# A conditioned hybrid decoder layer: nine pairs of up-projection tiles by half-size products in place of seven

## The chip, the cores and the metric

The kernel runs on one core of one Trainium2 chip. The metric is the device time of one execution in microseconds, as the median of several runs. A core has five engines that work side by side, each through its own list of instructions in order: TensorE (PE in the profile; its weight loads, PEld, overlap its products), VectorE (DVE), ScalarE (ACT), GpSimd (POOL) and SyncE (SP). SP, ACT and POOL also issue DMA transfers. Where an instruction needs what another engine or a transfer makes, it waits for a semaphore, and all that stands behind it in the same list waits too.

## The reference

One decoder layer on 512 tokens of width 1024, in float32. The part in front (conditioning, the input projection, two kinds of attention heads) is left out here. What matters is the end:

```python
mix = jnp.concatenate([o_hg, o_nsa], axis=-1) @ w_out[l]
x = x + gt1 * mix
h2 = rmsnorm(x, norm2_g[l]) * (1.0 + sc2) + sh2
u = causal_dwconv(h2 @ w_up[l], conv_w[l], conv_b[l])   # 1024 -> 5632, width 3
a, v = jnp.split(u, 2, axis=-1)
x = x + gt2 * ((jax.nn.silu(a) * v) @ w_down[l])        # 2816 -> 1024
```

`gt2` is one of six parts of `silu(c) @ w_ada + b_ada`, a row of 1024 numbers that the kernel spreads over 128 partitions. It is called the gate below.

## The kernel before

**Exact products from three.** A float32 operand is split into a rounded part `hi` (ACT copies it to a 32-bit format with fewer digits, L152) and the rest `lo` (DVE subtracts, L153). Each product of two such operands is three TensorE instructions (`mm3`, L155 to L158). Making `hi` and `lo` is called making a form. Some forms are made the other way ("added", L259 to L261 and L1694 to L1696): ACT writes the negated source into `lo`, and a DMA issued on POOL adds the source to it.

**The up-projection.** The 5632 output columns are 44 tiles of 128 columns, numbered `st` = 0 to 43. Two neighbours (an even one for `a`, an odd one for `v`) make one part `f` of the 22 parts of the hidden layer. A plain tile takes 8 blocks of the width by 3 products of 512 tokens, 24 products. After a tile, `up_post` (L1626) runs the width-3 convolution on ACT and DVE, the silu, and the product of the two.

From tile 8 on the tiles come in units of four (`j` is the unit's number, its tiles are `4j` to `4j+3`). In a unit the first two tiles are computed together by seven products of half size (a Strassen-Winograd scheme over halves of the width, of the tokens and of the two tiles). Tokens P1 to P7 stand for them. Each is 4 blocks by 3 products of 256 tokens, 84 in all in place of 96 half-size ones. They need sums of the inputs (`hS`, made once) and sums of the weights (`wq`, `e`, made for each unit by DVE). The other two tiles are plain, cut in two pieces each (tokens B0, B1, C0, C1).

**The order is written out by hand.** `PRO` (L46) is the order of the prologue (tiles 0 to 7) and `UNIT` (L47) that of a unit. Each token is a call in `do_` (L1745): M3 is the products of tile 3, q1 the `up_post` of tile 1, F6 and A5 the form of tile 6 and the added form of tile 5, p2 the `up_post` of the unit's third tile, m0' and m1' the forms of the next unit's two plain tiles, n1' to f7' the sums and forms of the next unit's weights, t a sum of inputs, x one item of the list `work`, g a step of the gate. An engine's instructions stay in the order in which the tokens make them. Before, units 2 to 8 come (`NU = 8`), and then a loop of eight plain tiles, 36 to 43, in which the digits of `PLAIN` say how many steps of the gate follow each tile.

**Work after a tile.** For each pair of parts, `g_parts` (L1818) puts sums and forms for the down-projection on the list `work`. `step` takes from it. The last item, `park` (L1845), stores what there is no room for in HBM. `gran`, the pool that holds most of this, has 33 slots, called granules. For the pairs named in `AWAY`, one more granule, `gQ`, is parked.

**The gate.** `ada_last` (L1399) is a generator. Each half of the gate is 8 blocks of 128 rows of `w_ada`, loaded one at a time (256 KB) and added up by DVE (L1410, L1415, L1420). Then comes a split into `hi` and `lo`, two products that add over the partitions (L1426, L1427) and a copy by ACT. In the first half each load goes into one buffer and so follows the DVE instruction that read the block before.

**The down-projection** also has seven products of half size, in four phases. `forms` (L1875) makes the forms of its weights, and `look` (L1930) asks for the next one, three ahead of the products. `each_a` (L2032) is what is done beside the first phase, the return of the parked granules among it (`load_away`, L1896; the third phase's `load_s34`, L1891).

Of the kernel before, what the change touches and what calls it, by code (L numbers as in the profile page):

```python
# [20 lines left out]
P = 128  # L21
T = 512
NT = T // P
D = 1024
# [17 lines left out]
NU = 8  # L42
AWAY = (0, 1)
CUT = {"B": 6, "C": 7}
ADD = (1, 1)
PLAIN = "2 A1 1 1 A2 1 1 1"  # L46
PRO = ("t t g x M1 M2 t t t t F3 M3 F4 t A5 q0 M4 q1 q2 F6 q3 M5 M6 A7 x q4 g x q5 x t x n1' ns' f2' nc' n5' q6 na' g s4' m0' x x M7 m1' x f6' f7' x x x x f4'")  # L47
# [64 lines left out]
def hybrid_layer_kernel(ctx: ExitStack, tc: tile.TileContext, d: dict, out: bass.AP, dbg=None):  # L112
# [1165 lines left out]
    def hg_mix(i):  # L1278
# [13 lines left out]
        rstd(r[:, 0:4], s[:, 0:4], 1.0 / P, 4.0 * EPS)  # L1292
        on = TMP([P, 4, P], tag="on")
# [4 lines left out]
    def hg_flip(i):  # L1298
# [10 lines left out]
        split(m[:, 0], m[:, 1], t)  # L1309
# [89 lines left out]
    def ada_last(s, res):  # L1399
        for q in range(2):  # L1400
            acc = res[:, q * 512:(q + 1) * 512]
            c0 = s * D + q * 512
            gp.memset(acc, 0.0)
            sp.dma_start(acc[0:1], d["b_ada"][:, c0:c0 + 512])
            for k in range(KT if q else 0):
                raw = TMP([P, 512], tag="ada2r")
                sp.dma_start(raw, ada_view[:, k, c0:c0 + 512])
                if k:
                    yield
                    ve.scalar_tensor_tensor(acc, last, cs[:, k - 1:k], acc, ALU.mult, ALU.add)  # L1410
                last = raw
            for k in range(0 if q else KT):
                last = res[:, 512:]
                if k:
                    ve.scalar_tensor_tensor(acc, last, cs[:, k - 1:k], acc, ALU.mult, ALU.add)  # L1415
                sp.dma_start(last, ada_view[:, k, c0:c0 + 512])
                if k < KT - 1:
                    yield
            yield
# [3 lines left out]
            split(hi, lo, acc)  # L1423
            yield
# [4 lines left out]
            yield  # L1429

# [146 lines left out]
    for i in range(NT):  # L1577
        x1.append(G([D], s="x1"))
        sp.dma_start(x1[i], x_view[:, i])
    next(gate1)  # L1580
# [6 lines left out]
    hg_mix(2)  # L1587
# [7 lines left out]
    hg_flip(2)  # L1595
# [20 lines left out]
    def up_mm(st, sl, ks=range(KT)):  # L1616
        if st not in us:
            us[st] = PS("u")
            if st not in wts:
                wts[st] = next_parts(st < nst - 2, added=st >= 4 * NU + 4 and PLAIN.split()[st - 4 * NU - 4][0] == "A")  # L1620
# [114 lines left out]
    def do(j, tok):  # L1735
        last = j == NU
        if tok.endswith("'"):
            if last:
                if tok in ("n1'", "m0'"):
                    piece()  # L1740
# [4 lines left out]
    def do_(j, tok):  # L1745
        lo_, hi_ = lo_half, hi_half
        w = forms7.get(j)
        u = partial(u_of, j)
        if tok == "P1":
            banks(j)  # L1750
            sprod(u(1, lo_), w[1], h2_quarter(0, lo_), True)
        elif tok == "P5":
# [25 lines left out]
        elif tok == "g":  # L1778
            next(ada2, None)
# [164 lines left out]
    gt2 = wp.tile([P, D], F32, tag="xin", name="gt2", bufs=1)  # L1944
# [165 lines left out]
```

## Time and profile before

| what | value |
|---|---|
| median of 3 runs | 674.73 us (674.34 to 675.54) |
| the profiled execution's own time | 674.35 us |
| its span, first to last instruction | 672.6 us |
| TensorE busy | 664.9 us (99%), 3999 products |
| VectorE busy | 577.8 us (86%) |
| ScalarE busy | 392.6 us (58%) |
| GpSimd busy | 60.0 us (9%) |
| moved by DMA | 128.52 MB, mean 191 GB/s |
| granted TensorE clock | 1.000 |

The stages by time from the start of the span: the attention heads end near 271 us; the output projection and the second normalization run to about 327 us; the up-projection's prologue to 372 us; seven units to 520 us; eight plain tiles to 564 us; the down-projection to 669 us.

How to read a row of the timeline: start in us, length in us, engine, line of the kernel, operation, output and inputs by the program's names, shape, count, and in brackets how long the engine had been idle and what ended that. The starts of neighbouring TensorE rows say what a product costs, since products overlap: the length of a row is longer than its step to the next. In the view by windows each row is one stretch: its length, then the busy time and count of instructions of PE, PEld, DVE, ACT and POOL, the granted clock, the share of time that the 16 DMA engines were busy, and GB/s.

### The profile page before, as it was taken

What the parts mean: (1) busy time and instruction counts of PE and PEld (TensorE: products, weight loads), DVE (VectorE), ACT (ScalarE), POOL (GpSimd) and SP (SyncE); (2) the same over time, 40 slices, a digit from 0 to 9 for tenths busy, and PEclk for the clock granted to TensorE, in tenths of its full rate; (3) what the DMA queues carried; (4) which work ended last, traced back from release to release, by engine and by line L of the source; (5) the groups of instructions that cost most, each with busy time, mean ns of one, the idle gap of its engine ahead of it and who ended that gap; (6) DMA issues with size and microseconds to landing.
All of it is one profiled execution on the core that took longest, in us unless ns stands there. A gap on an engine that the chain in (4) does not pass through costs nothing.

```text
span 672.6 us, 10869 instructions
## 1 busy us (share of the span) xinstructions
PE 664.9 (99%) x3999; PEld 565.1 (84%) x3999; DVE 577.8 (86%) x1155; ACT 392.6 (58%) x757; POOL 60.0 (9%) x80
## 2 busy tenths in 40 slices
PE   8999999999999999999999999999999999999998
PEld 4678898788898889888998888989888888888886
DVE  5688988999998997687878988998898789988787
ACT  5564446666677688335665766667675455553431
POOL 1006144200000000200000011010110000000000
PEclk9999999999999999999999999999999999999999
DMA  9998444388042132435436677986779773979932
GB/s 279 287 322 269 145 157 138 106 288 254 11 147 95 33 107 99 172 96 161 140 95 172 179 196 198 242 218 175 187 181 277 217 234 124 393 259 398 388 112 94
DMA packets 110473, 128.52 MB, mean 191 GB/s; under 512 B 7067, under 2 KB 84691, under 8 KB 110421
## 3 DMA queue, kind: packets, MB, share of 16 engines
q1 hardware_dynamic: 103541, 106.89, 51.1%
q0 software_dynamic: 2448, 8.91, 6.9%
q10 hardware_dynamic: 4432, 12.04, 4.7%
q8 instruction: 31, 0.51, 0.3%
q14 instruction: 21, 0.17, 0.1%
HBM read 105.01 MB, written 13.90 MB: 177 GB/s over the span
## 4 chain that ended last, share of the span: by engine, by line
PE 92%; SPq 3%; DMA 2%; DVE 1%; issue 0%; ACTq 0%; ACT 0%
PE u L156 11%; PE u L158 11%; PE u L157 11%; PE dn L157 5%; PE dn L156 5%; PE dn L158 5%; PE pT L156 3%; PE pT L158 3%; PE pT L157 3%; PE F L1059 3%; PE oT L1087 3%; PE oh L158 2%; PE oh L156 2%; PE oh L157 2%; SPq L317 2%; PE lev L1188 2%
## 5 line engine op out<-in xcount | busy, mean ns | idle before, releaser
L156 PE MATMUL u<-h2h,whi 128*128 128x512 f32 (+1 forms) x208 | 78.0, 375 | 0.0
L157 PE MATMUL u<-h2l,whi 128*128 128x512 f32 (+1 forms) x208 | 77.8, 374 | 0.0
L158 PE MATMUL u<-h2h,wlo 128*128 128x512 f32 (+1 forms) x208 | 77.6, 373 | 0.0
L153 DVE TENSOR_TENSOR wlo<-raw,whi 128x1024 fp32r<-128x1024 f32 (+1 forms) x38 | 44.5, 1170 | 6.7 <-ACT whi L152 6.5
L152 ACT CAST whi<-raw 128x1024 fp32r<-128x1024 f32 (+1 forms) x38 | 38.3, 1008 | 18.8 <-PE u L157 7.3
L158 PEld LDWEIGHTS u<-h2h,wlo 128*128 128x128 f32 x208 | 39.2, 188 | 7.5 <-DVE wlo L153 0.4
L156 PEld LDWEIGHTS u<-h2h,whi 128*128 128x128 f32 x208 | 39.3, 189 | 6.0
L157 PEld LDWEIGHTS u<-h2l,whi 128*128 128x128 f32 x208 | 39.3, 189 | 5.8
L1027 ACT ACTIVATE pt<-pt,mx 128x128 f32<-128x128 f32 (+3 forms) x64 | 35.9, 562 | 11.8 <-DVE mx L1011 10.7
L1634 DVE SCALAR_TENSOR_TENSOR y<-u,cv,y 128x511 f32<-128x511 f32 x44 | 32.8, 745 | 11.4 <-ACT y L1633 11.4
L156 PE MATMUL pT<-hT,whi 128*128 128x512 f32 x96 | 39.2, 408 | 0.0
L1638 ACT ACTIVATE y<-y 128x512 f32<-128x512 f32 x21 | 13.3, 633 | 42.0 <-DVE y L1635 42.0
L158 PE MATMUL pT<-hT,wlo 128*128 128x512 f32 x96 | 37.7, 393 | 0.0
L157 PE MATMUL pT<-hT,whi 128*128 128x512 f32 x96 | 37.6, 391 | 0.0
L1011 DVE CUSTOM_DVE_ANT_0 pt<-S,cmask 128x128 f32<-128x128 f32 (+3 forms) x64 | 29.7, 484 | 6.5 <-PE S L1006 6.3
L1066 ACT COPY pT<-F 128x512 f32<-128x512 f32 (+2 forms) x52 | 25.9, 503 | 14.4 <-PE F L1059 11.2
L1635 DVE SCALAR_TENSOR_TENSOR y<-u,cv,y 128x510 f32<-128x510 f32 x44 | 32.9, 749 | 1.6
L1633 ACT ACTIVATE y<-u,cv 128x512 f32<-128x512 f32 x44 | 33.8, 771 | 0.0
L393 POOL TENSOR_TENSOR hrs<-hrs,mhalf 128x4 f32<-128x4 f32 (+2 forms) x16 | 20.0, 1259 | 136.4 <-DVE hrs L392 136.3
L157 PE MATMUL u<-h2l,w 128*128 128x256 f32 (+1 forms) x84 | 28.0, 333 | 0.0
L156 PE MATMUL u<-h2h,w 128*128 128x256 f32 (+1 forms) x84 | 28.0, 333 | 0.0
L158 PE MATMUL u<-h2h,w 128*128 128x256 f32 (+1 forms) x84 | 28.0, 333 | 0.0
(456 smaller groups left out, 2079.2 us busy)
## 6 DMA issues: line engine op xcount, KB each, us to landing
raw<-in_w_up SPq DMA_DIRECT2D x44, 512.0 KB, 5.6
aw<-in_w_ada SPq DMA_DIRECT2D x24, 512.0 KB, 3.6
raw<-in_w_down SPq DMA_DIRECT2D x10, 1024.0 KB
ada<-in_w_ada SPq DMA_DIRECT2D x32, 256.0 KB, 5.8
wlo<-raw POOLq DMA_DIRECT2D x15, 512.0 KB, 4.6
raw<-in_w_in SPq DMA_DIRECT2D x7, 1024.0 KB, 6.1
rawd<-in_w_down SPq DMA_DIRECT2D x12, 512.0 KB, 10.3
pk<-st ACTq DMA_DIRECT2D x11, 512.0 KB, 4.0
```

What stands on the lines that cost most here:

```text
L152: sc.copy(hi, src)
L153: (eng or ve).tensor_tensor(lo, src, f32(hi), ALU.subtract)
L156: pe.matmul(o, ah, bh, start=start, stop=False, skip_group_check=True)
L157: pe.matmul(o, ah, bl, start=False, stop=False, skip_group_check=True)
L158: pe.matmul(o, al, bh, start=False, stop=stop, skip_group_check=True)
L1011: ve.tensor_tensor_reduce(pt[:, sl], ps[:, sl], cmask[:, 512 - W:512], -1.0, 1e30, ALU.add, ALU.min, mx[:, e:e + 1])
L1027: sc.activation(pt[:, sl], pt[:, sl], AF.Exp, bias=mx[:, e:e + 1], scale=-1.0, accum_out=su[:, h % 2, e:e + 1])
L1059: pe.transpose(ps[:, j * P:(j + 1) * P], src[:, j * P:(j + 1) * P], ident)
L1066: sc.copy(pT, ps[:, 0:n * P])
L1633: sc.activation(y, u, AF.Identity, bias=cv[:, 132 + c:133 + c], scale=cv[:, 88 + c:89 + c])
L1634: ve.scalar_tensor_tensor(y[:, 1:], u[:, :T - 1], cv[:, 44 + c:45 + c], y[:, 1:], ALU.mult, ALU.add)
L1635: ve.scalar_tensor_tensor(y[:, 2:], u[:, :T - 2], cv[:, c:c + 1], y[:, 2:], ALU.mult, ALU.add)
```

## The change

- `NU` becomes 10: tiles 36 to 43 are two more units (9 and 10) and the loop of plain tiles goes. In the last unit the tokens of the next unit do nothing, except that n1' and m0' now each call `look`, so down's first forms are made there. P1 of the last unit has one more product.
- `AWAY` becomes six pairs. Six `gQ` granules are parked; in down's first phase `each_a` brings them back, two at each odd step from the third on.
- The gate starts earlier. Its first half is loaded by POOL in place of SP. Seven of its eight blocks are worked in during the output projection (inside `hg_mix` and `hg_flip`, and around `out_norm`), the last block, the split and the products in three tokens g of the prologue. The second half has one step of g in each of the nine units, and its blocks go into a part of the constants that is no longer used.
- The silu of tile 42 is made in the last unit and no more in `each_a`.

```diff
-NU = 8
-AWAY = (0, 1)
+NU = 10
+AWAY = (0, 1, 2, 3, 4, 5)
-PLAIN = "2 A1 1 1 A2 1 1 1"
-PRO = ("t t g x M1 M2 t t t t F3 M3 F4 t A5 q0 M4 q1 q2 F6 q3 M5 M6 A7 x q4 g x q5 x t x n1' ns' f2' nc' n5' q6 na' g s4' m0' x x M7 m1' x f6' f7' x x x x f4'")
+PLAIN = ""
+PRO = ("t t x M1 M2 t t t t F3 M3 F4 t A5 g q0 M4 g q1 q2 g F6 q3 M5 M6 A7 x q4 x q5 x t x n1' ns' f2' nc' n5' q6 na' s4' m0' x x M7 m1' x f6' f7' x x x x f4'")
...
-    def hg_mix(i):
+    def hg_mix(i, between=lambda: None):
...
         rstd(r[:, 0:4], s[:, 0:4], 1.0 / P, 4.0 * EPS)
+        between()
         on = TMP([P, 4, P], tag="on")
...
-    def hg_flip(i):
+    def hg_flip(i, between=lambda: None):
...
-        split(m[:, 0], m[:, 1], t)
+        sc.copy(m[:, 0], t)
+        between()
+        ve.tensor_tensor(m[:, 1], t, f32(m[:, 0]), ALU.subtract)
...
     def ada_last(s, res):
         for q in range(2):
             acc = res[:, q * 512:(q + 1) * 512]
+            last = cb[:, C_LMASK:C_LMASK + 512] if q else res[:, 512:]
             c0 = s * D + q * 512
             gp.memset(acc, 0.0)
-            sp.dma_start(acc[0:1], d["b_ada"][:, c0:c0 + 512])
-            for k in range(KT if q else 0):
-                raw = TMP([P, 512], tag="ada2r")
-                sp.dma_start(raw, ada_view[:, k, c0:c0 + 512])
-                if k:
-                    yield
-                    ve.scalar_tensor_tensor(acc, last, cs[:, k - 1:k], acc, ALU.mult, ALU.add)
-                last = raw
-            for k in range(0 if q else KT):
-                last = res[:, 512:]
+            gp.dma_start(acc[0:1], d["b_ada"][:, c0:c0 + 512])
+            for k in range(KT):
                 if k:
                     ve.scalar_tensor_tensor(acc, last, cs[:, k - 1:k], acc, ALU.mult, ALU.add)
-                sp.dma_start(last, ada_view[:, k, c0:c0 + 512])
-                if k < KT - 1:
-                    yield
-            yield
+                yield
+                (sp if q else gp).dma_start(last, ada_view[:, k, c0:c0 + 512])
+                yield
             ve.scalar_tensor_tensor(acc, last, cs[:, k:k + 1], acc, ALU.mult, ALU.add)
             hi = TMP([P, 512], F32R, tag="rhi")
             lo = TMP([P, 512], F32R, tag="rlo")
             split(hi, lo, acc)
             yield
+            yield
             ps = PS()
...
             sc.copy(acc, ps)
             yield
+            yield
+
+    def gate_step(n=2):
+        for _ in range(n):
+            next(ada2, None)
...
+    gt2 = wp.tile([P, D], F32, tag="xin", name="gt2", bufs=1)
+    ada2 = ada_last(5, gt2)
+    gate_step()
     next(gate1)
     hg_mix(0)
...
-    hg_mix(2)
+    hg_mix(2, partial(gate_step, 1))
+    gate_step(1)
     hg_mix(3)
...
-    hg_flip(2)
+    hg_flip(2, partial(gate_step, 1))
+    gate_step(1)
...
                 if tok in ("n1'", "m0'"):
-                    piece()
+                    look()
...
             sprod(u(1, lo_), w[1], h2_quarter(0, lo_), True)
+            if last:
+                pe.matmul(u(1, hi_), w[1][0][:, 0], h2_quarter(0, lo_)[0][0], start=False, stop=False,
+                          skip_group_check=True)
...
         elif tok == "g":
-            next(ada2, None)
+            gate_step()
...
         sc.dma_start(x1d[:, i], x1[i])
+        gate_step(1)
         out_norm(i)
+        gate_step(1)
...
-    first = 4 * NU + 4
-    for st in range(first, nst):
-        up_mm(st, full)
-        if st >= nst - 2:
-            look()
-        if st == first:
-            up_post(st - 1)
-        elif st > first + 1:
-            up_post(st - 2)
-        for _ in range(int(PLAIN.split()[st - first][-1])):
-            next(ada2, None)
+    gate_step()
+    assert next(ada2, 0) == 0
     look()
-    up_post(nst - 2, False)
...
     def each_a(k):
         if k == 0:
-            sc.activation(ys[nst - 2], ys[nst - 2], AF.Silu)
+            pass
...
             step(3)
-            load_away(k // 2 - 1)
+            load_away(k - 3)
+            load_away(k - 2)
```

More of the change, by code (lines that the diff above doesn't have):

```diff
@@ L1619, in up_mm @@
             if st not in wts:
-                wts[st] = next_parts(st < nst - 2, added=st >= 4 * NU + 4 and PLAIN.split()[st - 4 * NU - 4][0] == "A")
+                wts[st] = next_parts(st < nst - 2, added=False)
         hi, lo = wts[st]
@@ L1745, in do_ @@
     def do_(j, tok):
+        last = j == NU
         lo_, hi_ = lo_half, hi_half
@@ L1942, in dn_out @@
         sp.dma_start(out_view[:, i, cols], t)
-    gt2 = wp.tile([P, D], F32, tag="xin", name="gt2", bufs=1)
-    ada2 = ada_last(5, gt2)
     lo_half, hi_half, full = slice(0, 256), slice(256, 512), slice(0, 512)
```

## The prediction

> **What bounds the kernel now.** I read the page first, for which engine is full, then the matrix engine's rows in order of time, to see whether it ever stands still after 260 us, and then the vector, scalar and POOL rows around the one place where it does.
>
> ```profile
> span 672.6 us, 10869 instructions
> PE 664.9 (99%) x3999; PEld 565.1 (84%) x3999; DVE 577.8 (86%) x1155; ACT 392.6 (58%) x757; POOL 60.0 (9%) x80
> ```
>
> TensorE is busy for 99% of the span, so what counts is its number of products and every place where another engine makes it wait. The next rows give the price of four tiles of the up-projection in both ways. They are the first product of a unit, the first of the next unit, the first plain tile, and the end of the plain tiles.
>
> ```profile
> 456.69 0.28 PE L156 MATMUL u<-h2h,w 128*128 128x256 f32 x1
> ...
> 477.72 0.28 PE L156 MATMUL u<-h2h,w 128*128 128x256 f32 x1
> ...
> 520.23 0.40 PE L156 MATMUL u<-h2h,w 128*128 128x512 f32 x1
> ...
> 563.76 0.39 PE L1426 MATMUL ps<-rhi,onesr 128*128 128x512 f32 x1
> 563.98 0.39 PE L1427 MATMUL ps<-rlo,onesr 128*128 128x512 f32 x1
> 564.21 0.39 PE L156 MATMUL dn<-whi,gP 128*128 128x512 f32 x1
> ```
>
> A unit takes 477.72 - 456.69 = 21.03 us. The eight plain tiles take 563.76 - 520.23 = 43.53 us, or 21.77 for four. That is exactly 192 products at 0.227 us (the spacing of the last rows), so the plain tiles have no stall to win back. The only stall of this length that I find in the up-projection is at the first plain tile inside the first unit (token B0 of unit 2):
>
> ```profile
> 375.07 0.28 PE L158 MATMUL ux<-hS,w 128*128 128x256 f32 x1
> 375.19 0.40 PE L156 MATMUL u<-h2h,whi 128*128 128x512 f32 x1
> 375.42 0.40 PE L157 MATMUL u<-h2l,whi 128*128 128x512 f32 x1
> 375.82 0.50 PE L158 MATMUL u<-h2h,wlo 128*128 128x512 f32 x1
> ```
>
> The third product comes 0.17 us late, at 375.82. It reads `wlo`, which the vector engine begins at 374.55 and ends 1.22 us later, at 375.77. So the vector engine's list ahead of this point has **no slack**: whatever delays it between 346 and 375 us delays TensorE, and a TensorE that never idles afterwards doesn't get the time back.
>
> ```profile
> 345.86 1.22 DVE L153 TENSOR_TENSOR hS<-hB,hS 128x1024 fp32r<-128x1024 f32 x1
> 348.00 0.75 DVE L1634 SCALAR_TENSOR_TENSOR y<-u,cv,y 128x511 f32<-128x511 f32 x1 [0.92 <-ACT y L1633]
> 348.78 0.75 DVE L1635 SCALAR_TENSOR_TENSOR y<-u,cv,y 128x510 f32<-128x510 f32 x1
> 352.23 0.75 DVE L1634 SCALAR_TENSOR_TENSOR y<-u,cv,y 128x511 f32<-128x511 f32 x1 [2.70 <-ACT y L1633]
> ...
> 357.64 1.23 DVE L153 TENSOR_TENSOR w<-raw,w 128x1024 fp32r<-128x1024 f32 x1 [1.70 <-ACT w L152]
> ...
> 362.73 0.74 DVE L1415 SCALAR_TENSOR_TENSOR gt<-gt,cs 128x512 f32<-128x512 f32 x1
> ...
> 364.25 0.75 DVE L1634 SCALAR_TENSOR_TENSOR y<-u,cv,y 128x511 f32<-128x511 f32 x1 [0.43 <-ACT y L1633]
> ...
> 373.28 0.75 DVE L1415 SCALAR_TENSOR_TENSOR gt<-gt,cs 128x512 f32<-128x512 f32 x1
> 373.94 0.69 DVE L1685 TENSOR_TENSOR raw<-raw 128x512 f32<-128x512 f32 x1
> 374.55 1.22 DVE L153 TENSOR_TENSOR wlo<-raw,whi 128x1024 fp32r<-128x1024 f32 x1
> ```
>
> **The gain.** Eight plain tiles become two units: 2 x (21.77 - 21.03) = 1.47 us. The last unit has one extra product of 256 columns in P1. That is 0.12 us, the step from 375.07 to 375.19. So 1.35 us is won on TensorE if nothing waits. The gate's four products are moved, not removed.
>
> **The out-projection's gate steps** (seven of the eight blocks of the gate's first half) I cost at nothing. Each is one vector multiply-add of 0.74 us (the row at 362.73) put into a wait that is there:
>
> ```profile
> 314.30 0.69 DVE L1510 TENSOR_TENSOR x<-x,tmp 128x512 f32<-128x512 f32 x1
> 315.78 0.16 DVE L1515 TENSOR_TENSOR ss<-ss 128x1 f32<-128x1 f32 x1 [0.79 <-ACT sq L1512]
> ...
> 317.32 0.48 DVE L1522 TENSOR_SCALAR hx<-x,rs 128x512 f32<-128x512 f32 x1
> ...
> 319.71 0.81 PE L1532 MATMUL ps<-cb,hx 128*128 128x128 f32 x6
> ```
>
> The vector engine waits 0.79 us for the square, and 0.74 fits in it. If a block's load isn't there, what waits behind is `hx`, and TensorE's transposes of it. The two halves of `hx` (0.48 us each from 317.32) are ready near 318.3 and TensorE reaches the transposes at 319.71, so 1.4 us of lateness is free. The bounds are 0 and about 1 us; I take 0, since each load is issued one row block earlier, on a POOL queue that is idle there.
>
> **The gate's last block, in the prologue**, is the step that decides. The new order is `A5 g q0 M4 g q1 q2 g F6`. The first g makes the seventh multiply-add and issues the load of the eighth block (k=7) on POOL. The second g needs that block, with only q0 between them. The first multiply-add hides: it follows `hS`, from 347.00 to 347.74, in the 0.92 us gap. POOL can then issue the load at about 347.85, just behind A5's transfer:
>
> ```profile
> 346.69 1.08 POOL L260 DMA_DIRECT2D wlo<-raw  x1 [15.45 <-ACT wlo L259]
> ```
>
> The vector engine ends q0 at 349.5 and stands at the second g until the block lands. Call that time L. Behind it in order wait: ACT's rounding copy `rhi`, ACT's `y` of q1, and with it all of q1, q2, F6 and what follows. The handovers are these, from the later occurrence of the same step and from q1 as it is now:
>
> ```profile
> 558.58 0.74 DVE L1420 SCALAR_TENSOR_TENSOR gt<-ada2r,cs,gt 128x512 f32<-128x512 f32 x1
> ...
> 559.36 0.62 ACT L152 CAST rhi<-gt 128x512 fp32r<-128x512 f32 x1
> ...
> 564.41 0.59 ACT L1428 COPY gt<-ps 128x512 f32<-128x512 f32 x1 [1.88 <-PE ps L1427]
> 564.89 1.06 ACT L152 CAST whi<-raw 128x1024 fp32r<-128x1024 f32 x1
> ...
> 351.44 1.43 ACT L1633 ACTIVATE y<-u,cv 128x512 f32<-128x512 f32 x2
> ```
>
> The multiply-add starts at L + 0.05, and `rhi` 0.78 later (558.58 to 559.36). ACT's `y` comes 0.57 after that (just under the 0.62 of `rhi`), and the vector engine's first operation of q1 another 0.79 later (351.44 to 352.23): L + 2.2 in all, against 352.23 now. The third g puts the copy of the gate between q2's silu and F6's form on ACT, 0.48 us (564.41 to 564.89). F6's row is ACT-bound already (its 1.70 us gap), so everything from there on is late by L + 2.2 + 0.48 - 352.23 = L - 349.55. Two multiply-adds leave the later list. The one at 362.73 gives nothing, since the row after it waits for ACT anyway (the 0.43 gap). The one at 373.28 gives 0.66. So `wlo` is late by **L - 350.2**, and TensorE with it, the gate's two products (0.46 us) being swallowed in that wait. Later the same 0.46 us is missing from unit 8. Net change: L - 350.2 - 0.46 - 1.35 = **L - 352.0**, with a floor of -1.35.
>
> **When does the block land?** No row shows a 256 KB load on POOL's queue, nor two transfers outstanding on it.
>
> ```profile
> gt<-in_w_ada SPq DMA_DIRECT2D x8, 256.0 KB, 2.8
> ...
> 332.10:334.10 2.00, 2.00 (x20) 2.00 (x19) 1.76 (x6) 1.02 (x4) 0.00 (x0) 1.00 0.49 132
> 349.40:352.20 2.80, 2.80 (x14) 2.31 (x13) 0.13 (x1) 2.58 (x4) 0.00 (x0) 1.00 1.07 217
> 352.20:353.60 1.40, 1.40 (x8) 1.17 (x7) 1.33 (x2) 0.67 (x2) 0.00 (x0) 1.00 0.04 6
> ```
>
> Lower end: it behaves as the same load does on SP's queue, 2.8 us from issue, so L = 347.85 + 2.8 = 350.65. Upper end: A5's 512 KB keep the DMA engines full until 352.2 (share 1.07, then 0.04), and the block goes after them. Alone, such a load spreads over 2.0 us at half the engines' time (332.10 to 334.10, share 0.49), and about 0.3 us more to the landing: L = 354.5. If its reads run ahead behind A5's transfer, 1.0 us of full engines would do, L = 353.5. Since the windows show the engines full until 352.2, I take the order of issue and L = 353.8.
>
> [...]
>
> **The rest of the change.** Units 3 to 7 each park 512 KB more. Units 2 and 3 already do that with no stall, and I cost it at nothing. In the last unit the next unit's forms are missing, so its looks at down's forms are covered. In down's first phase 2.1 MB more have to come back:
>
> ```profile
> 569.00:594.00 25.00, 25.00 (x112) 20.71 (x111) 22.59 (x30) 13.86 (x20) 0.00 (x0) 1.00 1.01 391
> ...
> 573.45 6.64 SPq L223 DMA_DIRECT2D raw<-in_w_down  x2
> ...
> 590.15 1.22 DVE L1867 TENSOR_TENSOR keep<-raw,keep 128x1024 f32<-128x1024 f32 x1
> ```
>
> The DMA engines are full there, so at 391 GB/s this is 5.4 us of delay on the queue. The weights issued at 573.45 are first used at 590.15, 16.7 us later, so I cost it at 0 (bounds 0 and 5.4).
>
> **The sum.** -1.35 + (353.8 - 350.2) - 0.46 = +1.8 us. The profiled execution took 674.35 (span 672.6 and 1.75 around it) and the median of the runs is 674.73, a difference of 0.06%. On the median: **676.5 us**. What a measurement can tell from no change is 0.2%, or 1.35 us.
>
> **The rivals.**
> - *The load is alone on its way* (ends on the other side). It lands as on SP's queue, L = 350.65. Then `wlo` is 0.45 late, which is the 0.46 that TensorE spends on the gate's products, and the full gain stays: **673.4 us**. It decides from L below 350.7. For it: 2.8 us in eight loads. Against it: A5's transfer is ahead and fills the engines.
> - *It overlaps with A5's but is slower than on SP*: L between 351 and 352.7, net -1.0 to +0.7, about **674.6 us**, not to be told from no change. For it: the engines may alternate between packets of the two. Against it: one transfer at a time is all that the trace shows.
> - *Down's first phase starves*: the parked granules come ahead of weights. All 5.4 us on TensorE's path, over the full gain, would give **678.8 us**, and with the prologue's loss more. Against it: the 16.7 us.
> - *The change doesn't do what it says*: in units 9 and 10 the vector engine falls behind and a unit costs as much as four plain tiles. Then 1.47 are missing, **678 us** with the prologue's loss. Against it: seven units run without a stall.
>
> **How the numbers follow.** The forecast has 0.50 (its own range 675.4 to 677.2, from L 352.7 to 354.5), the overlap 0.22, the lone load 0.15, starving 0.06, slow units 0.07. Faster by over 0.2% needs nearly the whole gain: 0.12, most of the lone load. Slower by over 0.2% needs L above 353.4 or one of the last two: 0.50. No change: 0.38. The range reaches from the lone load to the slow units, 673.3 to 677.8.
>
> **What would show it.** Right: the vector engine idles some 4 us before a row `gt<-...,cs` near 354, released by a DMA; the first B0's third product comes about 3.6 us later than 375.82; units stay at 21.03 us to the last; nothing waits from 570 to 600 us. Wrong: that idle time under 2 us and B0's `wlo` on time; or waits of products on `whi` in down's first phase.

## The result, and the profile after

The changed kernel takes **684.53 us** (median of 4 runs, 684.13 to 684.90), the kernel before on the same chip 674.54 us (4 runs, 673.99 to 675.54): a ratio of 1.0139, 95% interval 1.0123 to 1.0156. It is 10 us slower; I had said 2. The page of the changed kernel, and under it the chain line of the kernel before:

```profile
span 682.4 us, 11063 instructions
PE 668.9 (98%) x4072; PEld 567.7 (83%) x4072; DVE 585.3 (86%) x1175; ACT 398.9 (58%) x773; POOL 68.3 (10%) x92
PE 66%; DVE 11%; ACT 9%; DMA 7%; SPq 4%; issue 2%; ACTq 0%; DVEq 0%
```

```profile
PE 92%; SPq 3%; DMA 2%; DVE 1%; issue 0%; ACTq 0%; ACT 0%
```

The busy shares hardly moved. The chain that ended last did: TensorE held 92% of it, now 66%, the rest being DVE, ACT and DMA. So the loss is waiting, spread over several places. Following TensorE's rows from 327 us to the end gives three.

**First, the prologue.** VectorE's list where it stands at the second g of the prologue, and TensorE's first plain tile in the first unit (B0):

```profile
353.68 0.75 DVE L1415 SCALAR_TENSOR_TENSOR gt<-gt,cs 128x512 f32<-128x512 f32 x1 [3.95 <-DMA gt<-in_w_ada]
```

```profile
378.52 0.50 PE L156 MATMUL u<-h2h,whi 128*128 128x512 f32 x1 [1.64 <-ACT whi L152]
...
379.78 0.80 PE L158 MATMUL u<-h2h,wlo 128*128 128x512 f32 x1 [0.53 <-DVE wlo L153]
380.38 0.63 PE L156 MATMUL u<-h2h,whi 128*128 128x512 f32 x1
380.80 0.63 PE L157 MATMUL u<-h2l,whi 128*128 128x512 f32 x1
...
383.27 0.40 PE L157 MATMUL u<-h2l,whi 128*128 128x512 f32 x1
```

The block lands at about 353.6 (predicted 353.8), VectorE has idled 3.95 us, and B0's third product comes at 379.78 in place of 375.82: **3.96 us** (0.2 of it was there at the up-projection's first product). But the next products step by 0.42 us, not 0.227. The view by windows says why (the first number behind the five busy times is the granted clock):

```profile
380.00:382.00 2.00, 2.00 (x5) 1.60 (x6) 2.00 (x6) 2.00 (x6) 0.87 (x1) 0.50 0.27 51
382.00:384.00 2.00, 2.00 (x8) 1.55 (x7) 1.97 (x5) 1.81 (x5) 0.00 (x0) 0.71 1.09 207
384.00:386.00 2.00, 2.00 (x14) 1.79 (x13) 1.49 (x3) 1.01 (x3) 0.00 (x0) 1.00 0.94 362
```

After the wait TensorE ran at half clock (0.50) for about 3.4 us. Eight steps take 383.27 - 379.78 = 3.49 us in place of 8 x 0.227 = 1.82: **1.7 us** more.

**Second, the units.** The first products of token P5 in units 5 and 6, and the place in between where TensorE waits (the first product of P6, which needs token S):

```profile
442.92 0.28 PE L156 MATMUL ux<-hS,w 128*128 128x256 f32 x1
...
448.24 0.39 PE L158 MATMUL u<-h2h,wlo 128*128 128x512 f32 x1
449.24 0.39 PE L156 MATMUL u<-hS,wq 128*128 128x256 f32 x1 [0.61 <-ACT u L1777]
...
465.05 0.28 PE L156 MATMUL ux<-hS,w 128*128 128x256 f32 x1
```

A unit takes 465.05 - 442.92 = 22.13 us, not 21.03; TensorE waits for ACT's copy L1777 (S). From the same rows of the other units, units 4 to 8 take 21.30, 22.13, 21.73, 22.19 and 21.60 us: **3.8 us** over 21.03 in all. The cause starts earlier. SyncE's rows for the first pair of raw weight loads of each unit, after and then before:

```profile
386.37 1.14 SPq L223 DMA_DIRECT2D raw<-in_w_up  x2
...
408.53 1.16 SPq L223 DMA_DIRECT2D raw<-in_w_up  x2
...
431.23 1.38 SPq L223 DMA_DIRECT2D raw<-in_w_up  x2
...
453.36 1.37 SPq L223 DMA_DIRECT2D raw<-in_w_up  x2
```

```profile
403.25 1.13 SPq L223 DMA_DIRECT2D raw<-in_w_up  x2
...
424.30 1.99 SPq L223 DMA_DIRECT2D raw<-in_w_up  x2
...
444.92 1.08 SPq L223 DMA_DIRECT2D raw<-in_w_up  x2
```

The loads came every 20.6 to 21.1 us before; after, they come every 22.1 to 22.7 us from the first unit on. The loop from a raw load over its forms to the release of its buffer has become longer than a unit. TensorE lives on its lead through unit 3 and then waits in each unit to the eighth.

**Third, down's first phase**, TensorE and VectorE rows in order of time:

```profile
576.88 1.22 DVE L1871 TENSOR_TENSOR keep<-raw 128x1024 f32<-128x1024 f32 x1
...
578.01 1.21 DVE L153 TENSOR_TENSOR wlo<-raw,whi 128x1024 fp32r<-128x1024 f32 x1
...
579.28 0.50 PE L157 MATMUL dn<-wlo,gP 128*128 128x512 f32 x1 [1.46 <-DVE wlo L153]
```

The third form stands in VectorE's list behind what is left of the last unit, and TensorE waits for its `wlo`. The down-projection takes **1.8 us** longer (from its first product to the start of its last: 106.67 against 104.87).

The sum: 3.96 + 1.7 + 3.8 + 1.8, less the 1.35 won and the 0.46 of the gate's products that unit 8 no longer holds, with 0.3 in small rests, is 9.8 us. That is the difference of the two spans (682.4 - 672.6).

### The profile page after: what moved, and what is told of

Read it like the earlier page. It is cut to its first block, busy times and chain, and to the rows that moved or that the text cites. A ratio compares the mean times of both kernels' runs of the same rounds, so it can differ in the third digit from the quotient of the medians.

```text
span 682.4 us, 11063 instructions
## 1 busy us (share of the span) xinstructions
PE 668.9 (98%) x4072; PEld 567.7 (83%) x4072; DVE 585.3 (86%) x1175; ACT 398.9 (58%) x773; POOL 68.3 (10%) x92
## 4 chain that ended last, share of the span: by engine, by line
PE 66%; DVE 11%; ACT 9%; DMA 7%; SPq 4%; issue 2%; ACTq 0%; DVEq 0%
PE dn L157 5%; PE dn L158 5%; PE dn L156 5%; DMA raw<-in_w_up 4%; PE u L158 4%; PE u L156 4%; PE u L157 4%; PE pT L156 3%; PE pT L158 3%; PE pT L157 3%; PE F L1059 3%; PE oT L1087 3%; DVE y L1641 3%; DVE y L1640 2%; SPq L317 2%
## 5 line engine op out<-in xcount | busy, mean ns | idle before, releaser
L156 PE MATMUL u<-h2h,whi 128*128 128x512 f32 (+1 forms) x200 | 75.7, 378 | 1.6 <-ACT whi L152 1.6
L158 PE MATMUL u<-h2h,wlo 128*128 128x512 f32 (+1 forms) x200 | 75.4, 377 | 0.5 <-DVE wlo L153 0.5
L157 PE MATMUL u<-h2l,whi 128*128 128x512 f32 (+1 forms) x200 | 75.3, 376 | 0.0
L153 DVE TENSOR_TENSOR wlo<-raw,whi 128x1024 fp32r<-128x1024 f32 (+1 forms) x32 | 37.2, 1161 | 4.6 <-ACT whi L152 4.5
L152 ACT CAST whi<-raw 128x1024 fp32r<-128x1024 f32 (+1 forms) x32 | 32.0, 999 | 11.7 <-PE kva L158 4.4
L152 ACT CAST wq<-raw 128x512 fp32r<-128x512 f32 x45 | 27.7, 618 | 14.5 <-DVE w L153 11.2
L156 PE MATMUL u<-hS,wq 128*128 128x256 f32 x108 | 31.3, 290 | 1.6 <-ACT u L1777 1.6
L153 DVE TENSOR_TENSOR wq<-raw,wq 128x512 fp32r<-128x512 f32 x45 | 30.7, 684 | 2.2 <-ACT wq L152 2.2
```

Of the source, the lines that this page charges most:

```text
L152: sc.copy(hi, src)
L153: (eng or ve).tensor_tensor(lo, src, f32(hi), ALU.subtract)
L156: pe.matmul(o, ah, bh, start=start, stop=False, skip_group_check=True)
L157: pe.matmul(o, ah, bl, start=False, stop=False, skip_group_check=True)
L158: pe.matmul(o, al, bh, start=False, stop=stop, skip_group_check=True)
```

## The experiments

Each was timed in rounds with the kernel before on the same chip (674.6 to 675.0 us, ratios with 95% intervals).

### Is it the gate or the parks?

`e5_parks_only` is the kernel before with only the six parked granules:

```diff
-AWAY = (0, 1)
+AWAY = (0, 1, 2, 3, 4, 5)
...
-            load_away(k // 2 - 1)
+            load_away(k - 3)
+            load_away(k - 2)
```

> The kernel before (eight plain tiles, gate as before) with six granules parked in place of two and brought back as in the changed kernel. If the parks alone make the units slow: units 4 to 8 have stalls as in the changed kernel, about 3 us in all, 677.5 us, and down's first phase has no stall beside it. If the units are slow because of what the prologue left behind: no stall, 674.5 us.

Measured: 678.64 us (677.89 to 679.64), ratio 1.0058 [1.0043, 1.0073]. Units 5 to 7 take 21.13, 21.97 and 21.74 us, and TensorE waits again in unit 8 (0.93 us). By the trace 3.1 us of the loss lie in units 5 to 8, and 0.8 ahead of the up-projection, where the two kernels are the same. So the parks alone cost 3 to 4 us, with no gate step moved and no unit added.

`e6_gate_only` is the kernel before (`NU = 8`, two parks, plain tiles at the end) with the changed kernel's gate and `PRO`:

> The kernel before with the gate as in the changed kernel (block loads by POOL, seven blocks in the output projection, the eighth and the products in the prologue, the rest in units and plain tiles), seven units and two parks. Theory: the stall at B0 of unit 2 is all there, the third product near 379.6, 3.6 to 4 us late, with or without a stretch of half clock (1.7 us); units at 21.03; 678 us without and 679.7 with the half clock. Rival (the prologue's stall needs the nine units or the six parks): 674.7.

Measured: 680.22 us (677.98 to 680.36), 1.0074 [1.0056, 1.0092]. All its units after the first take 21.03 us, except one of 21.39. B0's wait is the same as in the changed kernel (1.65 and 0.53 us). The gate's place alone costs some 5.5 us with the half clock; the one run at 677.98, 3.3 us above the kernel before, is the one at the highest granted clock (0.999 against 0.996 and 0.997), and its profile shows no half clock at B0. So each half of the loss is there without the other: 5.5 and 4.0, with 1.8 of down and -1.35 for the two further units, add up to some 10 us. That the sum comes out does not make them independent, as the next two runs show.

### The prologue

`e1_swap` and `e2_early` move the step g that issues the eighth block, ahead of A5's transfer:

```diff
-F4 t A5 g q0 M4
+F4 t g A5 q0 M4     (e1_swap)
+F4 g t A5 q0 M4     (e2_early)
```

> The changed kernel with one swap in the prologue: 'g A5' in place of 'A5 g', so POOL issues the load of the gate's eighth block ahead of A5's adding transfer. Theory (the block waits behind A5's transfer on POOL's queue): the load lands near 351 in place of 353.7, TensorE waits under 1 us at B0 of unit 2 in place of 2.6, does not drop to half clock, and the kernel takes about 679.5 us, 5 less than the changed kernel. Rival (the load takes some 5 us whatever stands ahead of it, because the engines are full): it lands near 353.5 again and the time stays at 684.5.

> The changed kernel with the first g two tokens earlier ('F4 g t A5 q0' in place of 'F4 t A5 g q0'): the seventh multiply-add and the load of the eighth block come about 1.2 us sooner and ahead of A5's transfer. Theory for the prologue: the block is there when the second g asks for it, the vector engine waits under 1 us, no stall at B0, no half clock, 5.5 us less than the changed kernel, 679.0 us. For the units there are rivals: if units 4 to 10 are slow because of the six parks (on ACT's list or by their traffic), they still lose 4 us and 679 holds; if they are slow because they inherit the vector engine's delay from the prologue, they run at 21.03 again and the kernel takes 675.

Measured: 681.13 us (679.04 to 682.23), 1.009 [1.0071, 1.011], and 681.25 us (680.15 to 682.10), 1.0095 [1.008, 1.011]: both some 3.3 us better than the changed kernel. POOL's rows in `e2_early`, and B0's two waits:

```profile
347.20 0.54 POOL L1413 DMA_DIRECT2D gt<-in_w_ada  x1 [15.65 <-DVE gt L1411]
347.87 0.93 POOL L260 DMA_DIRECT2D wlo<-raw  x1
...
376.18 0.50 PE L156 MATMUL u<-h2h,whi 128*128 128x512 f32 x1 [0.18 <-ACT whi L152]
377.44 0.50 PE L158 MATMUL u<-h2h,wlo 128*128 128x512 f32 x1 [0.53 <-DVE wlo L153]
```

Issued ahead of A5, the block takes 4.1 us to land; behind A5, in the changed kernel, 5.3 us. In `e1_swap` it is issued later and lands 2.9 us after that, near the 2.8 us of the loads on SyncE's queue. POOL's issue there, and VectorE's wait:

```profile
348.96 0.54 POOL L1413 DMA_DIRECT2D gt<-in_w_ada  x1 [16.79 <-DVE gt L1411]
...
351.92 0.75 DVE L1415 SCALAR_TENSOR_TENSOR gt<-gt,cs 128x512 f32<-128x512 f32 x1 [1.56 <-DMA gt<-in_w_ada]
```

POOL's queue is not slow in itself (2.9 us against 2.8). VectorE still waits 1.6 us in both runs, and B0's third product comes 1.4 us later than in the kernel before, counted from the first product of the up-projection; no half clock follows. So a load as fast as on SyncE's queue, issued 0.3 us later than the rival of the lone load assumed, does not keep the full gain that this rival promised.

Both runs missed their forecasts of 679.5 and 679.0 us, and the units show why: units 4 to 8 lose 5.2 and 5.1 us in place of 3.8. Part of what TensorE no longer waits at B0 it waits in the units, where the raw loads set the pace.

### Why the parks cost

The parks ride on ACT, three stores in a row in a unit where there were two. My first theory was ACT's own time: the third issue takes 1.07 us, where the two stores of a unit without a park take 0.33 each, 1.9 us apart, and behind it stands f3, the form whose last reader releases the raw buffer. Five runs move the store.

`e3_park_sp` gives it to SyncE, `e4_park_later` leaves it on ACT, one work item later and so behind f3:

```diff
-            sc.dma_start(pk26[:, AWAY.index(j)], f32(gQ.pop(j)))
+            sp.dma_start(pk26[:, AWAY.index(j)], f32(gQ.pop(j)))     (e3_park_sp)
+            late.append(j)           (e4_park_later; issued by ACT in the next call of step)
```

> The changed kernel with the store of the parked granule gQ issued by SP in place of ACT, at the same token; bytes and moment stay. Theory (three DMA issues in a row hold up ACT's list ahead of f3, and with it the vector engine and the next raw load): units 4 to 8 run at 21.03 us, the 4 us come back, about 681 us. Rival (the extra 0.5 MB a unit slow the loads of the weights): nothing changes, 684.5. The stall at B0 of unit 2 and the half clock stay in both.

> The changed kernel with the store of gQ still issued by ACT, but one item of the work list later, behind the unit's form f3. Bytes, queue and ACT's total stay. Theory (what counts is that the third DMA issue stands ahead of f3 in ACT's list, since f3 frees the buffer of the next raw load): units 4 to 8 come back to 21.03 us or near, about 681 us. Rival (it is ACT's total, or any three issues close together): the units stay slow, 684.5.

Measured: `e3_park_sp` 678.24 us (677.48 to 679.02), 1.0052 [1.0035, 1.0069], with every unit after the first at 21.03 but one of 21.43. The forecast was 681 us; beyond the units, three of its four runs and its profile have no half clock (granted clock 0.999 and 1.000), which is worth 1.7 us, and down's products take 106.03 us in place of 106.67. `e4_park_later` 685.76 us (683.24 to 686.18), 1.0156 [1.0135, 1.0176], units of up to 22.66: no better than the changed kernel. A store that no longer delays f3 should have been better. **That theory falls**, at least as far as f3 goes.

What remained were two: ACT's time for the issue wherever it stands, or the store's bytes against the raw loads. In `e4_park_later` the store goes out 2.0 us ahead of SyncE's raw loads in place of 3.4; with SyncE it stands behind them in the same queue. `g1_park_pool` gives the store to GpSimd at the same place, and `h1_park_after_loads` was to put it behind the loads on ACT (ahead of up_post(p-1)):

```diff
+            gp.dma_start(pk26[:, AWAY.index(j)], f32(gQ.pop(j)))     (g1_park_pool)
...
+            late.append(j)           (h1_park_after_loads, h2_park_behind)
...
         elif tok[0] == "p":
+            if tok == "p-1":         (h1_park_after_loads; "p2" in h2_park_behind)
+                while late:
+                    q = late.pop()
+                    sc.dma_start(pk26[:, AWAY.index(q)], f32(gQ.pop(q)))
```

> The changed kernel, with the parked granule stored by GpSimd at the place in its list where ScalarE did it, so ScalarE issues two stores in a row as before the change, and the store still goes out ahead of the raw loads on a queue of its own. Theory A (bytes ahead of the raw loads): the loads land in 6 us or later, units of 21.5 to 22 us, 682 to 685 us; if the store comes to stand behind the accumulate in GpSimd's queue and so behind the raw loads, 677.5 to 679. Theory B (ScalarE's three issues in a row, the third at 1.08 us for 0.33): units of 21.03 us, 677.5 to 679.0 us.

> The changed kernel, with ScalarE's store of the parked granule issued some 10 us later, ahead of up_post(p-1), when SyncE has issued all four raw loads of the unit. Between the two kernels so far, only the store's place against the raw loads differs from the run that parks by SyncE (there it stands behind the loads in the same queue, and the loads land in 5.2 us; in the changed kernel it stands ahead of them by 3.4 us and they land in 6.2; with the store one item later, 2.0 us ahead, in 7.2). Theory A, the store's 512 KB are served ahead of the next raw loads by the same DMA engines: here the loads land in about 5.2 us again, the units take 21.03 to 21.1 us, and the time is near that of the SyncE store, 677.5 to 679.0 us. Theory B, the cost is ScalarE's own time for the issue, wherever it stands: units of 21.5 to 22.3 us as in the changed kernel, 683 to 686 us.

Measured: `g1_park_pool` 685.70 us (684.54 to 687.15), 1.0163 [1.0146, 1.0181], units up to 23.0; `h1_park_after_loads` 684.17 us (683.61 to 685.26), 1.0137 [1.012, 1.0154], units of 21.85 to 22.07. In the first ACT issues two stores again, at 0.33 us each, and nothing is better: **the theory of ACT's time falls whole**. The second looks like a point for it, but the DMA issues of one unit say otherwise:

```profile
449.36 0.33 ACTq L1863 DMA_DIRECT2D pk<-st  x1
451.24 0.33 ACTq L1864 DMA_DIRECT2D pk<-st  x1
453.05 0.33 ACTq L1788 DMA_DIRECT2D pk<-gQ  x1
453.64 1.33 SPq L223 DMA_DIRECT2D raw<-in_w_up  x2
```

The store went out 0.6 us ahead of the loads, not behind: I had put the step too early. And three stores on ACT that are 1.9 us apart take 0.33 us each, with no gain. `h2_park_behind` is the same edit at p2:

> The changed kernel, with ScalarE's store of the parked granule issued ahead of up_post(p2), by the trace some 8 us later than in the last such run, where it went out at 453.05 us and the first raw load at 453.64: it was still ahead of the loads. Here it goes out at about 460 us, when all four raw loads have been issued (453.6 to 459.1) and the first pair has landed. Theory A, the store's 512 KB on a queue of their own share the DMA engines with the raw loads that come right after: gone here; the first raw loads land in about 5.2 us, units of 21.03 to 21.2 us, 677.5 to 679.5 us. Theory C, in whatever place, a store outside SyncE's queue takes the time from some load of the same unit (here the accumulate onto wlo, 459.8 to 466.5 us): units of 21.5 us or more, 681 to 686 us.

Measured: 679.14 us (677.15 to 679.87), 1.006 [1.0045, 1.0074]. The same unit's DMA issues, and the first products of P5 in units 5 and 6:

```profile
448.15 0.33 ACTq L1864 DMA_DIRECT2D pk<-st  x1
450.56 1.96 SPq L223 DMA_DIRECT2D raw<-in_w_up  x2
...
453.30 3.12 SPq L223 DMA_DIRECT2D raw<-in_w_up  x2
455.03 0.33 ACTq L1788 DMA_DIRECT2D pk<-gQ  x1
```

```profile
443.06 0.28 PE L156 MATMUL ux<-hS,w 128*128 128x256 f32 x1
...
464.09 0.28 PE L156 MATMUL ux<-hS,w 128*128 128x256 f32 x1
```

Every unit after the first takes 21.03 us. Same engine, same instruction, same bytes; only its place against the raw loads differs. The stores' cost is shown to be their place **ahead of the raw loads on another queue**. How the loads feel it is told by ACT's first form of a unit's raw loads, which waits for the first of them. In unit 5 that load is issued at 453.36 in the changed kernel, at 453.64 in `h1_park_after_loads` and at 450.56 in `h2_park_behind` (rows above). ACT's form starts, in this order, at:

```profile
458.33 1.06 ACT L1700 ACTIVATE wlo<-raw 128x1024 fp32r<-128x1024 f32 x1 [2.24 <-DMA raw<-in_w_up]
```

```profile
459.22 1.06 ACT L1700 ACTIVATE wlo<-raw 128x1024 fp32r<-128x1024 f32 x1 [3.42 <-DMA raw<-in_w_up]
```

```profile
454.99 1.06 ACT L1700 ACTIVATE wlo<-raw 128x1024 fp32r<-128x1024 f32 x1 [2.27 <-DMA raw<-in_w_up]
```

That is 4.97, 5.58 and 4.43 us after the issue. Over units 3 to 7 it is 4.9 to 5.9 us in the changed kernel, 5.6 to 5.9 in `h1_park_after_loads` and 6.0 to 6.7 in `g1_park_pool`, where the store is ahead; where it is behind, 4.1 to 4.6 in `h2_park_behind` and 4.2 to 5.2 in `e3_park_sp`. (The 5.2, 6.2 and 7.2 us in the expectations are medians of the view of DMA issues. It gives a landing for few of these loads, 6 of 28 in the changed kernel and one in `e3_park_sp`, so they don't compare like with like.) The DMA engines are full in that part of a unit (share 0.92 to 1.19 in windows of 4 us from 448 to 464 us of the changed kernel), which fits my reading that 512 KB ahead of the loads come out of their time: the first load comes late whether ACT or GpSimd issues the store ahead of it (4.9 to 5.9 and 6.0 to 6.7 us, against 4.1 to 5.2 behind).

### The third look

`e7_look` asks for down's third form at m1' of the last unit rather than after it:

```diff
-                if tok in ("n1'", "m0'"):
+                if tok in ("n1'", "m0'", "m1'"):
...
     assert next(ada2, 0) == 0
-    look()
```

> The changed kernel with the third of down's first forms made in the last unit (at token m1') in place of after it. Theory (the third form stands behind the last unit's leftover work in the vector engine's list): the wait of 1.6 us for wlo at the third product step of down's first phase goes, 683 us. Rival (the wait is for the weights' load in the full DMA queue): it stays, 684.5.

Measured: 682.83 us (681.33 to 683.76), 1.0125 [1.0108, 1.0142]. Of TensorE's wait in down's first phase (1.46 us before the row at 579.28) this is left:

```profile
576.01 0.50 PE L157 MATMUL dn<-wlo,gP 128*128 128x512 f32 x1 [0.18 <-DVE wlo L153]
```

Down's products take 105.85 us in place of 106.67: 0.8 of the 1.8 us back. What is left of the 1.8 is this product and another at 584.66, each late for a `wlo` by some 0.45 us with the one behind it. The forecast of 683 us was met with the help of the clock: three of the four runs were granted 0.999 or 1.000, all four of the changed kernel 0.997 or 0.998.

### A version without the stalls

All three repairs together (park by SyncE, third look at m1', and the whole gate one block earlier, so that the prologue has only its last steps) make a kernel that should keep the gain. Three versions of it differ in where a further step of the gate, meant for the subtraction of its last half, stands in the last unit: nowhere, with the subtraction after the unit (`e8_best`), at ns' (`f1_best`), at s4' (`f3_best`). The edits beside those above, in short:

```diff
-t A5 g q0 M4 g q1 q2 g F6
+t A5 i q0 M4 q1 i q2 i F6
...
-f2' nc' n5' q6 na'
+f2' nc' n5' i q6 na'
...
+        elif tok == "i":
+            gate_step(1)
...
-    hg_mix(0)
+    hg_mix(0, partial(gate_step, 1))
+    gate_step(1)
...
                 if tok in ("n1'", "m0'", "m1'"):
                     look()
+                if tok == "s4'":     (f3_best; "ns'" in f1_best)
+                    gate_step(1)
```

In the generator the copy to `hi`, the subtraction for `lo`, and the products with their copy became one step each.

> The changed kernel with all three causes taken out: gQ stored by SP; the third of down's first forms at m1'; the gate one block earlier (a step also in the first head mix), so that the prologue holds only the eighth multiply-add, the copy, the subtraction and the products, each at a place where its engine waits anyway. If the three causes are the whole story, the gain of 1.35 us is left: 673.4 us. If something else in nine units costs time, it stays above 674.7.

> The changed kernel with four edits: parked granules stored by SyncE; third look at down's forms at m1' of the last unit; gate one block earlier through hg_mix(0) and single steps; and, new against the run with the first three and the gate, the subtraction for the gate's last half at ns' of the last unit instead of after it. That run had no stall from 340 to 562 us and then one of 7.5 us at the gate's last product, with half clock behind it. If this was only the order of the subtraction, the stall is gone: about 673.1 us (672.5 to 674.0), 0.997 to 0.9985 of the kernel before. If the gate's product waits for something else as well, some 676 to 683 us.

> The changed kernel with parked granules stored by SyncE, the third look at m1' of the last unit, the gate one block earlier, and the subtraction for the gate's last half at s4' of the last unit, behind the step that makes its input. In the run with it at ns' the same step was the multiply-add of the last block, which waited 5.7 us for the block (landed at 555.6 us), and TensorE behind it 5.4 us and then at half clock for 6.8 us; all units took 21.03 us and down's products 104.87, as in the kernel before. Without that stall (5.4 us of gap and some 2.4 us of half clock of a span of 678.7): a span of about 671, so 672 to 673 us, 0.9955 to 0.998 of the kernel before. If the subtraction stalls VectorE again: 675 us or more.

`e8_best` took 682.96 us (682.55 to 683.22), 1.0122 [1.0106, 1.0137]; `f1_best` 680.22 us (679.80 to 680.90), 1.0082 [1.0067, 1.0097]; `f3_best` 674.25 us (673.84 to 675.01), 0.9991 [0.9982, 1.0]. All have every unit at 21.03 us, and each one stall of my own making. The rows, one from each in this order (for `f1_best` the VectorE row that it waits for, too):

```profile
570.02 0.79 PE L1425 MATMUL ps<-rlo,onesr 128*128 128x512 f32 x1 [7.35 <-DVE rlo L1421]
```

```profile
555.67 0.75 DVE L1415 SCALAR_TENSOR_TENSOR gt<-cb,cs,gt 128x512 f32<-128x512 f32 x1 [5.66 <-DMA cb<-in_w_ada]
...
557.42 0.58 PE L156 MATMUL u<-hS,wq 128*128 128x256 f32 x1 [5.24 <-DVE u L1785]
```

```profile
563.12 0.50 PE L1425 MATMUL ps<-rlo,onesr 128*128 128x512 f32 x1 [0.96 <-DVE rlo L1421]
```

In the first, the subtraction for the gate's last product stood behind the third look in VectorE's list. In the second I stepped the gate once more at ns', and that step was not the subtraction but the multiply-add of the last block, which hadn't landed. In the third it stood behind the tile before it. `f2_pool` and `f4_best_act` are `f1_best` with the store on GpSimd (ahead of the loads), and `f3_best` with the store on ACT at p2 (behind them):

> As the run f1_best, with GpSimd in place of SyncE storing the parked granule. Theory A: loads of 6 us again and units above 21.03 us, 675 to 678 us, unless the accumulate in GpSimd's queue holds the store back behind the raw loads; Theory B: no stall, the same 673.1 us (672.5 to 674.0) as f1_best.

> As the run f3_best, with ScalarE in place of SyncE storing the parked granule, ahead of up_post(p2), behind the raw loads. Theory A: the same as f3_best, 672 to 673 us, units of 21.03 us. Theory C: units of 21.5 us or more, 676 to 680 us.

Measured: `f2_pool` 688.80 us (688.21 to 689.18), 1.0207 [1.0192, 1.0223], units up to 23.07, 8.6 us above `f1_best`, 7.1 of them in the units (its forecast of 675 to 678 us had `f1_best` at 673); `f4_best_act` 674.44 us (673.79 to 675.01), 0.9993 [0.9985, 1.0002], all units 21.03 to 21.05. The finding on the parks holds in a kernel without the stall at B0. `f5_best` and `f6_best_act` are `f3_best` and `f4_best_act` with the subtraction directly behind its input in place of at s4', in a gap in which VectorE waits for ACT anyway:

```diff
         elif tok == "g":
-            gate_step()
+            gate_step(3 if last else 2)
```

> As f3_best, with the subtraction for the gate's last half one place earlier in the last unit: as the third step of the g there, in a gap of 1.37 us in which VectorE waits for ScalarE (558.1 to 559.46 us). In f3_best it came at 562.39 and TensorE waited 1.13 us between the gate's two last products (561.77 to 563.12); nothing else of the 18 pairs' up-projection stalled. Without that wait: f3_best less 1.1 us, 673.1 us (672.6 to 673.9), 0.9965 to 0.9985 of the kernel before. If something else is late there, no change, 674.2 us.

> As f4_best_act (parked granules stored by ScalarE behind the raw loads), with the same edit as f5_best: 673.3 us (672.7 to 674.0); without effect 674.4 us.

Measured: **673.55 us** (672.43 to 674.47), 0.9980 [0.9971, 0.9989], and **673.14 us** (672.62 to 674.18), 0.9982 [0.9973, 0.9990]: 11 runs each against 21 of the kernel before (674.63). Both are 11 us faster than the changed kernel, and faster than the kernel before by 0.2%, with intervals clear of 1. TensorE's rows in `f6_best_act`: the first product of P5 in the first unit, the same in the last, the gate's products, the first of down:

```profile
373.79 0.28 PE L156 MATMUL ux<-hS,w 128*128 128x256 f32 x1
...
542.12 0.28 PE L156 MATMUL ux<-hS,w 128*128 128x256 f32 x1
...
561.72 0.40 PE L1424 MATMUL ps<-rhi,onesr 128*128 128x512 f32 x1
561.96 0.39 PE L1425 MATMUL ps<-rlo,onesr 128*128 128x512 f32 x1
562.18 0.39 PE L156 MATMUL dn<-w,gP 128*128 128x512 f32 x1
```

Eight units take 542.12 - 373.79 = 168.33 us, which is 8 x 21.03 and the 0.12 of the extra product (less 0.03 of rounding), and TensorE shows no wait from 340 us to down's first product. In down's first phase one product (at 576.25) still comes 0.24 us late for a `wlo`, and the next another 0.11.

## Why the prediction was right or wrong

- *The gain of 1.35 us*: right. With all stalls gone, 0.2% of 674.63 is 1.35 us for `f5_best` and 1.2 us for `f6_best_act` (the medians differ by 1.1 and 1.5). In both traces it is 235.73 us from TensorE's first product of the up-projection to its first of down, 237.34 before: 1.61 us less, of which 0.28 is the wait at B0 that the kernel before had. Down's products give 0.4 back (105.3 against 104.87). The rival that the added units would be slower as such is out.
- *The block lands at L = 353.8*: right (353.6), and in part by luck: the load was issued at 348.34, 0.5 us later than assumed, and took 5.3 us rather than 6.0. "The order of issue" is borne out, as the load ahead of A5 lands in 2.9 and 4.1 us and the one behind it in 5.3.
- *"`wlo` is late by L - 350.2"*: 3.4 us by the measured L; the row says 3.96. What failed is the 0.66 us credited for the multiply-add that leaves VectorE's list at 373.28, since `wlo` also needs ACT's rounding copy `whi`. ACT's row in the kernel before, then ACT's and VectorE's in the changed kernel:

```profile
373.39 1.03 ACT L152 CAST whi<-raw 128x1024 fp32r<-128x1024 f32 x1
```

```profile
377.44 1.03 ACT L152 CAST whi<-raw 128x1024 fp32r<-128x1024 f32 x1
378.50 1.22 DVE L153 TENSOR_TENSOR wlo<-raw,whi 128x1024 fp32r<-128x1024 f32 x1 [0.37 <-ACT whi L152]
```

Before, `whi` ended at 374.42 and `wlo` began at 374.55, so 0.13 us was to be won, not 0.66. After, `whi` is 4.05 us late and VectorE waits for it. With 0.13 in the sum, `wlo` is late by L - 349.68, which is 3.95 us. The lone load, at L = 350.65, would have been late by 1.0 us and not 0.45, so that rival was priced 0.5 us too low.
- *No term for the clock*: the sum took it for given that a stalled TensorE goes on at full speed. In the profiled run of the changed kernel it doesn't: 1.7 us. The granted clock of the other three runs (0.997 and 0.998) says the same of them.
- *"Units 3 to 7 each park 512 KB more. Units 2 and 3 already do that with no stall, and I cost it at nothing"*: **the step that failed most**, at 3.8 us. Two units without a stall were no proof. In `e5_parks_only` TensorE waits no more in units 2 to 4 than in the kernel before, but the first loads of its units 2 to 6 come 20.93, 21.42, 22.03 and 21.98 us apart, and from unit 5 on TensorE follows. The loads fall behind first, and TensorE's lead covers it until it is used up.
- *"In the last unit the next unit's forms are missing, so its looks at down's forms are covered"*: two of them are; the third, behind the unit, wasn't: 1.8 us. Its place accounts for 0.8 (`e7_look`); 0.6 go when only the store is moved (106.03 us in `e3_park_sp` and `h2_park_behind`), so part of it is the units' lateness carried on.
- *The out-projection's steps at nothing*: right. From TensorE's first product of the last attention stage to that of the up-projection are 55.75 us, 55.73 before.
- *Down's first phase does not starve*: right. No wait on the returned granules; the waits are on a `wlo`.

So the side was right (slower), the size wrong by 8 us, and outside the range. The mechanism that I had given the largest share holds for 3.96 of the 9.8 us. Two signs named for being right, "units stay at 21.03 us to the last" and "nothing waits from 570 to 600 us", failed, and those are the two terms that I had put at nothing; the idle VectorE and the late B0 came as named.

Of the half clock one thing stays open: when it comes. The same wait at B0 (1.64 and 0.53 us in the changed kernel, 1.65 and 0.53 in `e6_gate_only`) is followed by it in the profiles of the changed kernel, h1, h2 and e4 (granted clock 0.997 and 0.998), and not in those of e3, e6, e7 and g1 (0.999 and 1.000).

## What to carry to other kernels

Before costing one more store at nothing, look whether the DMA engines are full where it goes out (here a share of 0.92 to 1.19), and which load comes next; a store that nobody waits for belongs behind the loads that someone waits for; here it made no difference whether ACT or SyncE issued it there (673.14 and 673.55 us). Two units without a stall don't prove that a loop keeps up: compare the period of its loads with the period of the bound engine, over more units than the lead lasts (here 22.1 to 22.7 us against 21.03). And when a stall of TensorE is costed, look at the granted clock behind it (here 0.50 for 3.4 us).

## What the runs showed of the hardware

- Behind the wait of 1.64 and 0.53 us with a little work between, TensorE ran at half clock in the changed kernel, from about 379.7 to 383.1 us (0.50 in the view by windows); behind nearly the same wait in `e6_gate_only` (1.65 and 0.53 us) it did not. Behind the waits of 5.24 us (`f1_best`) and 7.35 us (`e8_best`) the products were slow, too: those of 256 columns step by 0.21 us from 557.80 to 559.93, in place of 0.12, and those of 512 columns by 0.43 from 570.61 to 571.89, in place of 0.227. The granted clock of those two profiled runs was 0.995 and 0.994, that of `f3_best` 1.000. What wait is long enough for it was not shown.
- Three stores in a row on ACT took 0.33, 0.47 and 1.07 us to issue; stores 1.9 us apart took 0.33 each. On SyncE a store behind the loads took 1.9 to 3.1 us to issue in `e3_park_sp` and 1.8 to 3.1 in `f1_best`, and no unit of `f1_best` lost time by it (21.03 us each).
- A 256 KB load on POOL's queue took 2.9 and 4.1 us from issue to landing ahead of another transfer (`e1_swap`, `e2_early`) and 5.3 behind it; on SyncE's queue it was 2.8.
